# Six of eight conv channel tiles of an input projection as 2x2 block products, with attention results kept in DRAM

## The chip, the cores and the metric

The kernel runs on one core of a Trainium2 chip. The core has a matrix engine (TensorE, PE in the profile), three engines for elementwise work (VectorE is DVE, ScalarE is ACT, GpSimd is POOL), a synchronisation engine (SyncE, SP) that here only issues DMAs, an on-chip memory SBUF of 128 partitions, and PSUM, the matrix engine's accumulators. The metric is the device time of one execution in microseconds, lower is better.

## The reference

One layer of a hybrid decoder, in float32, for 512 tokens with 16 meta tokens put in front (L = 528), width 2048. What the change touches is the first half:

```python
n = _rmsnorm(h, g_mix[l])
p = n @ w_in[l]                      # 2048 -> 6 x 1024: q k v | b c u
q, k, v, gb, gc, u = jnp.split(p, ...)
o_attn = _stick_breaking_attention(norm(q), norm(k), v)   # 8 heads x 128
o_conv = gb * _causal_dwconv(gc * u, conv_w[l])           # 3 taps, 1024 channels
o = jnp.concatenate([_rmsnorm(o_attn, g_attn_out[l]),
                     _rmsnorm(o_conv, g_conv_out[l])], axis=-1)
h = h + o @ w_out[l]
n2 = _rmsnorm(h, g_ffn[l])
h = h + (jax.nn.silu(n2 @ w_gate[l]) * (n2 @ w_up[l])) @ w_down[l]
```

The FFN's inner width is 5632. The meta positions are dropped from the output.

## The kernel before, in words

**Layout and precision.** Activations are held transposed: 128 channels on the partitions, tokens along the row. A channel tile is 128 channels. To keep float32 precision on a faster matmul type, every operand is split into a high part (a cast to fp32r, on ScalarE) and a low part (the difference, on VectorE), and every product is three matmuls: high x high, high x low, low x high. So a weight block of 128 x 128 meets an activation of N tokens in three matmuls of N columns, and every weight passes once through ScalarE and once through VectorE.

**Input projection and attention.** x is scaled by g_mix and split into nh and nl, 16 tiles of 528 columns each (`split_x`, L236). `product` (L178, with `product_steps`, L162) runs over the 16 row tiles of one column tile of w_in, high and low weights from `next_w` (L141). `prepare` (L127) loads weights by SyncE, 1024 columns at a time into two buffers (raw), and splits 512 columns at a time into whi and wlo, four such pieces ahead. For each of eight heads (`head`, L337) the k, q and v column tiles are multiplied, and the attention of the head before is woven in: `after` (L151) puts a piece of work in a list, and `tick` (L154), called once per row tile, starts it when its count has run out. `mix` (L464) leaves a head's result, split, in its slot of oa, which stays in SBUF.

**Conv channels (L506 to L538).** For each of eight channel tiles j the column tiles c and u are multiplied for the tokens from 12 on (two halves of 258 columns, matmuls of 258) and b for the 512 real tokens (matmuls of 512). VectorE multiplies c by the square of the token's norm factor (L512), by u (L515), and adds the three taps (L517 to L522); b is scaled (L525), POOL multiplies (L526), and ScalarE and VectorE split the result into its slot of oc (L535, L536). The square is added up in acc_c for the norm.

**Output projection (L540 to L865).** The first output tile is multiplied with oa and oc by `product`; then the pools of the first half are released, and the pool sw is opened with other weight buffers: four of 1024 columns (b11, b12, b21, b22), three split pairs (s) and two sums. `wide_product` (L674) does the other 15 output tiles, and VectorE and POOL add the residual, build the FFN's activation blocks and store what does not fit. `scale_a` (L502) and `scale_c` (L775) turn the sums of squares into the two norm factors with two matmuls each (`token_scale`, L486).

**FFN as 2x2 blocks.** With the rows of a matrix in two halves, two column tiles, and the tokens in two halves, `pair_product` (L705) gets four block results from seven block products in place of eight. The activations come ready mixed in seven slots (f0 to f6, later ring and first); the weights' sums are made on the way: `prepare_pair` (L629) splits four blocks and three sums of blocks for the seven products and makes four additions of 1024 columns on VectorE (`add_quads`, L613). `block_product` (L685) is 8 row tiles x 3 matmuls of 256 columns; the results are combined from PSUM by three copies on ScalarE (L726 to L730) and three operations on VectorE (L732 to L739). 44 pairs make gate and up, 28 pairs the down projection (4 with 168 matmuls, 24 with 126).

**Order.** The code's order is only a start: the program is laid out by priority, so an engine's instructions may stand in another order than the code's, but each engine then runs its own list strictly in order. Weight preparation has high priority. All pools on the right side of SBUF are laid down from the top in the order in which they are opened: before, npool and wpool first, and after their release hpool (acc_h and 96 bytes named pad_h), sw, fpool (four of the f slots) and hbuf. A slot of activations starts 16 bytes into its tile.

Of the kernel before, what the change touches and what calls it, by code (L numbers as in the profile page):

```python
# [15 lines left out]
P = 128  # L16
# [17 lines left out]
def hybrid_layer(ctx: ExitStack, tc: tile.TileContext, xT, w_in, w_out, w_gu, w_down, vecs, out):  # L34
# [19 lines left out]
    tmp = open_pool("tmp", side="right")  # L54
# [5 lines left out]
    def t512(cols=SEQ, tag="t", bufs=6):  # L60
        n_tmp[0] += 1
        return tmp.tile([P, cols], F32, tag=tag, bufs=bufs, name=f"tmp{n_tmp[0]}")
# [39 lines left out]
    stream = []  # L102

    OUT_TILES = [k + 8 * half for k in range(8) for half in (1, 0)]

    def plan_w(src, n):
        stream.append((src, n))

    FIRST = ((0, 2), (2, 4), (4, 8), (8, 12), (12, 16))
    for a, b in FIRST:  # L110
        for c in (8, 0):
            plan_w(w_in[c, a // 8][:, (a % 8) * P : (a % 8 + b - a) * P], b - a)
    for j in range(HEADS):
        for c in (8 + j, j, 16 + j)[0 if j else 2 :]:
            for b in range(2):
                plan_w(w_in[c, b], 8)
    for j in range(HEADS):
        for c in (32 + j, 40 + j, 24 + j):
            for b in range(2):
                plan_w(w_in[c, b], 8)  # L120
    for b in range(2):
        plan_w(w_out[OUT_TILES[0], b], 8)
    raws, ready, taken = [], [], [0]
    SUB, AHEAD = 4, 4
    subs = [(i, a, min(a + SUB, n)) for i, (_, n) in enumerate(stream) for a in range(0, n, SUB)]

    def prepare():  # L127
        i, a, b = subs[len(ready)]
        with tc.high_priority():
            if i == len(raws):  # L130
                raws.append(wpool.tile([P, 8 * P], F32, tag="raw", bufs=2, name=f"raw{i}"))
                src, n = stream[i]
                nc.sync.dma_start(raws[i][:, : n * P], src)
            raw, c = raws[i][:, a * P : b * P], (b - a) * P
            hi = wpool.tile([P, SUB * P], F32R, tag="whi", bufs=AHEAD + 1, name=f"whi{i}_{a}")
            lo = wpool.tile([P, SUB * P], F32R, tag="wlo", bufs=AHEAD + 1, name=f"wlo{i}_{a}")
            sc.copy(hi[:, :c], raw)  # L137
            ve.tensor_tensor(lo[:, :c], raw, hi[:, :c].bitcast(F32), ALU.subtract)  # L138
        ready.append((hi, lo, b - a))

    def next_w():  # L141
        i = taken[0]
        taken[0] += 1
        while len(ready) < min(len(subs), i + 1 + AHEAD):
            prepare()
        hi, lo, n = ready[i]
# [936 lines left out]
```

## Time and profile before

| | |
|---|---|
| runs | 2111.97, 2111.64, 2109.75 us; median 2111.64 |
| profiled execution: span, first to last instruction | 2109.2 us (the page gives no other time of it) |
| granted TensorE clock, mean | 0.996 |
| instructions | 39231, of them 16086 matmuls |
| from HBM, to HBM | 268.60 MB, 71.30 MB |
| input projection and attention | about 0 to 347 us |
| conv channels | about 347 to 628.5 us |
| output projection | about 628.5 to 803 us |
| gate and up | about 805 to 1660 us |
| down projection | to the end |

How to read the rows: a name such as `pc<-nh,whi` is what an instruction writes and reads by the program's names (pk, pq, pv, pc, pu, pb are the projections' accumulators, po the output projection's, x, y, z those of the pairs). L512 is line 512 of the kernel. In the groups a row ends with the busy time, the mean length of one instruction in ns, and the idle time of its engine just before, with what ended it. Matmuls are pipelined, so their lengths overlap; the distance from start to start is what one costs.

### The profile page before, as it was taken

Reading aid. Unit: us, or ns where it says so; the run is one execution under the profiler, and the core shown is the slowest. Engines: PE = TensorE matmul, PEld = TensorE weight load, DVE = VectorE, ACT = ScalarE, POOL = GpSimd, SP = SyncE. Lnnn points to the kernel's source line nnn. Section 1 sums busy time; section 2 is a strip of 40 time slices with the busy share of each in tenths; the row PEclk is TensorE's granted clock in tenths of the full one; section 3 lists DMA queues with packets and bytes.
Section 4 is the critical chain, followed back from the end, with each engine's and each line's share of the span. In section 5 each row is a group of like instructions: output and inputs, shape, how many; then the busy total and the mean of one; then the engine's idle time right before and its main releaser. Section 6 shows DMA issues by size and latency. Waiting matters only on the chain.

```text
span 2109.2 us, 39231 instructions
## 1 busy us (share of the span) xinstructions
PE 2070.9 (98%) x16086; PEld 1989.7 (94%) x16086; DVE 1638.1 (78%) x2075; ACT 1013.5 (48%) x1532; POOL 470.2 (22%) x592
## 2 busy tenths in 40 slices
PE   8999999999999998999999999999999999999999
PEld 7999999999998888999999999999999999999999
DVE  8777767433337678899999998999989877776798
ACT  5666666322224344555544554554555544444443
POOL 4111111010013544122121121221111333122232
PEclk9999999999999999999999999999999999999999
DMA  5222222222235556566565565565554998788763
GB/s 173 80 71 80 71 80 81 81 93 98 91 113 170 180 181 215 166 183 192 156 185 170 152 193 166 164 182 158 171 155 145 319 298 244 218 244 242 222 191 120
DMA packets 147796, 342.47 MB, mean 162 GB/s; under 512 B 13136, under 2 KB 62800, under 8 KB 147616
## 3 DMA queue, kind: packets, MB, share of 16 engines
q1 hardware_dynamic: 69472, 216.17, 32.0%
q0 software_dynamic: 78144, 123.79, 21.9%
q8 instruction: 126, 2.06, 0.4%
q14 instruction: 54, 0.44, 0.1%
HBM read 268.60 MB, written 71.30 MB: 161 GB/s over the span
## 4 chain that ended last, share of the span: by engine, by line
PE 80%; DVE 8%; DMA 6%; issue 3%; ACT 2%; DVEq 0%; SPq 0%; ACTq 0%; POOL 0%
PE x L703 8%; PE x L701 8%; PE x L702 8%; DMA b<-w_down 4%; PE z L701 4%; PE z L702 4%; PE z L703 4%; DVE s L610 3%; PE po L681 3%; PE po L680 3%; PE po L682 3%; PE y L702 2%; PE y L703 2%; PE y L701 2%; PE pv L169 2%
## 5 line engine op out<-in xcount | busy, mean ns | idle before, releaser
L609 ACT CAST s<-t 128x1024 fp32r<-128x1024 f32 (+1 forms) x288 | 283.2, 983 | 403.5 <-PE x L703 132.3
L610 DVE TENSOR_TENSOR s<-t,s 128x1024 fp32r<-128x1024 f32 (+1 forms) x288 | 338.4, 1175 | 95.2 <-ACT s L609 94.7
L702 PE MATMUL x<-f,s 128*128 128x256 f32 x1408 | 388.1, 276 | 2.1 <-DVE f L184 1.3
L703 PE MATMUL x<-f,s 128*128 128x256 f32 x1408 | 388.1, 276 | 1.9 <-DVE s L610 1.9
L701 PE MATMUL x<-f,s 128*128 128x256 f32 x1408 | 388.1, 276 | 0.2 <-ACT f L183 0.2
L609 ACT CAST s<-b 128x1024 fp32r<-128x1024 f32 (+1 forms) x216 | 212.4, 983 | 217.5 <-PE x L703 196.1
L702 PEld LDWEIGHTS x<-f,s 128*128 128x128 f32 x1408 | 265.1, 188 | 2.5 <-DVE f L184 1.5
L703 PEld LDWEIGHTS x<-f,s 128*128 128x128 f32 x1408 | 265.0, 188 | 2.1 <-DVE s L610 2.1
L701 PEld LDWEIGHTS x<-f,s 128*128 128x128 f32 x1408 | 265.1, 188 | 0.5 <-ACT f L183 0.4
L610 DVE TENSOR_TENSOR s<-b,s 128x1024 fp32r<-128x1024 f32 (+1 forms) x216 | 245.5, 1137 | 5.6 <-ACT s L609 4.5
L138 DVE TENSOR_TENSOR wlo<-raw,whi 128x512 fp32r<-128x512 f32 (+1 forms) x198 | 142.3, 720 | 131.5 <-ACT whi L137 130.9
L896 POOL DMA_DIRECT2D fd<-s x147 | 104.1, 925 | 564.4 <-DVE s L184 562.9
L137 ACT CAST whi<-raw 128x512 fp32r<-128x512 f32 (+1 forms) x198 | 121.3, 614 | 186.7 <-PE pu L171 65.5
L701 PE MATMUL z<-f,s 128*128 128x256 f32 x704 | 195.8, 278 | 4.2 <-ACT sides L728 4.0
L703 PE MATMUL z<-f,s 128*128 128x256 f32 x704 | 193.9, 275 | 0.0
L702 PE MATMUL z<-f,s 128*128 128x256 f32 x704 | 193.9, 275 | 0.0
L616 DVE TENSOR_TENSOR t<-b,b 128x1024 f32<-128x1024 f32 (+1 forms) x144 | 165.1, 1146 | 36.2 <-DMA b<-w_down 32.8
L701 PE MATMUL x<-ring,s 128*128 128x256 f32 x608 | 168.5, 277 | 9.3 <-DVE d L736 5.7
L703 PE MATMUL x<-ring,s 128*128 128x256 f32 x608 | 168.0, 276 | 0.5 <-DVE s L610 0.5
L702 PE MATMUL x<-ring,s 128*128 128x256 f32 x608 | 167.5, 275 | 0.0
L701 PEld LDWEIGHTS z<-f,s 128*128 128x128 f32 x704 | 132.2, 188 | 7.4 <-ACT sides L728 7.4
L702 PEld LDWEIGHTS z<-f,s 128*128 128x128 f32 x704 | 132.2, 188 | 0.0
(350 smaller groups left out, 5695.3 us busy)
## 6 DMA issues: line engine op xcount, KB each, us to landing
b<-w_gu SPq DMA_DIRECT2D x176, 512.0 KB, 3.6
raw<-w_in SPq DMA_DIRECT2D x92, 512.0 KB, 3.4
fd<-s POOLq DMA_DIRECT2D x147, 256.0 KB, 5.3
b<-w_down SPq DMA_DIRECT2D x96, 384.0 KB, 4.8
ring<-fd POOLq DMA_DIRECT2D x42, 768.0 KB, 7.7
wide<-w_out SPq DMA_DIRECT2D x30, 512.0 KB, 3.7
hd<-d POOLq DMA_DIRECT2D x48, 256.0 KB, 7.7
b<-w_down SPq DMA_DIRECT2D x16, 512.0 KB, 7.6
```

The lines of the kernel that those rows point to most:

```text
L137: sc.copy(hi[:, :c], raw)
L138: ve.tensor_tensor(lo[:, :c], raw, hi[:, :c].bitcast(F32), ALU.subtract)
L609: sc.copy(hi, src)
L610: ve.tensor_tensor(lo, src, hi.bitcast(F32), ALU.subtract)
L616: ve.tensor_tensor(sums[name], a, b, ALU.add)
L680: pe.matmul(ps, hi[:, kk], ah, start=k == 0, stop=False)
L681: pe.matmul(ps, hi[:, kk], al, start=False, stop=False)
L682: pe.matmul(ps, lo[:, kk], ah, start=False, stop=k == 7)
L701: pe.matmul(p, hi[:, kk], act[:, 0, k], start=start and j == k == 0, stop=False, skip_group_check=skip)
L702: pe.matmul(p, hi[:, kk], act[:, 1, k], start=False, stop=False, skip_group_check=skip)
L703: pe.matmul(p, lo[:, kk], act[:, 0, k], start=False, stop=k == n - 1, skip_group_check=skip)
L896: gp.dma_start(fd[c][s][:, :, k], t[:, :, i])
```

## The change

Conv channel tiles 0 and 1 are multiplied as before (with 260 columns in place of 258). Tiles 2 to 7 go two at a time, as three pairs: (c, u) of the first, (c, u) of the second, (b, b) of both. Each is a `pair_product` over the 16 row tiles in two halves and the tokens from 8 on in two halves of 260, seven products of 8 row tiles.

The pairs need mixed activations. Three of the seven operands are parts of nh and nl as they are. Three blocks of differences (blk, split) are built during channel tile 1 by `form_blocks`, which loads x again; the seventh ("late") overwrites the second token half of the first eight nh and nl tiles after channel tile 1.

All weights of the kernel, from the first to the last, now pass through one plan and one set of buffers, those of sw, which is opened first: splits of 1024 columns, two ahead. The pool wpool and the reload between the two schemes go. Since blk and sw take the space that oa and oc had, each head's result and conv tiles 0 and 1 are written to DRAM when done (`stage_out`, one buffer), and loaded back by POOL's queue when blk has been read for the last time, in the last pair. The output projection starts with conv tiles 2 to 7 for two output tiles, then tiles 0 and 1, then the attention's eight. `scale_c` is handed to `after` ahead of these steps.

By the pools: hpool's pad_h (96 bytes) is gone, sw has a pad of 128 bytes at its lower end, hpool is opened below sw, and two tails of slots are shortened; the FFN's and the down projection's code is otherwise the same.

The diff, cut to its core:

```diff
+    sw = open_pool("sw", side="right")
+    sw.tile([P, 32], F32, name="pad_sw")
     npool = open_pool("npool", side="right")
-    wpool = open_pool("wpool", side="right")
...
+    CONV_FIRST = 2
+    def plan_pair(n, srcs, first=False):
+        i = len(pairs)
+        pairs.append((n, first))
+        for q in ("21", "11", "12", "22") if first else ("11", "12", "22", "21"):
+            loads.append(((i, q), n, srcs[("11", "12", "21", "22").index(q)]))
+        for s in (5, 0, 1, 2, 3, 4, 6) if first else range(7):
+            ents.append((i, s))
...
-    for j in range(HEADS):
+    for j in range(CONV_FIRST):
         for c in (32 + j, 40 + j, 24 + j):
             for b in range(2):
-                plan_w(w_in[c, b], 8)
+                plan_raw(w_in[c, b], 8)
+    for j in range(CONV_FIRST, HEADS, 2):
+        for c in ((32 + j, 40 + j), (33 + j, 41 + j), (24 + j, 25 + j)):
+            plan_pair(8, columns(c), not pairs)
...
+    S_AHEAD = 2
+    def split_quad(src, n):
+        t = sw.tile([P, 2, 8 * P], F32R, tag="s", bufs=S_AHEAD + 1, name=f"s{len(split_w)}")
+        hi, lo = (t[:, i, : n * P] for i in range(2))
+        sc.copy(hi, src)
+        ve.tensor_tensor(lo, src, hi.bitcast(F32), ALU.subtract)
...
+    def stage_out(name):
+        t = stage.tile([P, 2, SEQ], F32R, tag="st_o", name=f"st_{name}")
+        def store():
+            od[name] = dram.tile([P, 2, SEQ], F32R, name=f"od_{name}")
+            gp.dma_start(od[name], t)
+        return t[:, 0], t[:, 1], store
...
-    C0, CH = 12, (L - 12) // 2
+    C0, CH = 8, (L - 8) // 2
...
+            def form_blocks(k):
+                x4 = form.tile([P, 4, CH], F32, tag="x4", bufs=2, name=f"x4_{k}")
+                for i, kk in ((0, k), (2, k + 8)):
+                    nc.sync.dma_start(x4[:, i : i + 2], two(xT[kk][:, C0:]))
+                for i, kk in ((0, k), (2, k + 8)):
+                    sc.activation(x4[:, i : i + 2], x4[:, i : i + 2], AF.Copy, scale=g_mix[:, kk : kk + 1])
+                a11, a21, a12, a22 = (x4[:, i] for i in range(4))
+                ve.tensor_tensor(late[:, k], a11, a21, ALU.subtract)
+                ve.tensor_tensor(a22, a22, a21, ALU.subtract)
+                ve.scalar_tensor_tensor(a21, a22, -1.0, a11, ALU.mult, ALU.subtract)
+                ve.scalar_tensor_tensor(a12, a21, -1.0, a12, ALU.mult, ALU.subtract)
+                split(blk[:, :, 0, k], blk[:, :, 1, k], x4[:, 1:])
+            for k in range(8):
+                after(3 + 5 * k, lambda k=k: form_blocks(k))
...
+    for k in range(8):
+        hi, lo = (t[:, C0 + CH :] for t in n_hl[k])
+        split(hi, lo, late[:, k])
...
+    conv_acts = [
+        parts_of(0, C0), of_blk(2), of_blk(0), of_blk(1), parts_of(0, C0 + CH), parts_of(8, C0), parts_of(8, C0 + CH)
+    ]
...
+    def pair(acts):
+        c1, c2 = halves_of("e"), halves_of("e2")
+        x = pair_product(acts, two(c1), two(c2), sides)
+        sc.copy(two(c1)[:, 1], x)
+        return c1, c2
+
+    for j in range(CONV_FIRST, HEADS, 2):
+        ys = []
+        for m in range(2):
+            c1, c2 = pair(conv_acts)
+            ys.append(t512(SEQ, "v", 2)[:, :SEQ])
+            conv_taps(j + m, two(c1), two(c2), ys[m])
+        gbs = pair(conv_acts)
+        if j < HEADS - 2:
+            slots = [oc_mid[:, j + m - CONV_FIRST] for m in range(2)]
+        else:
+            cpool.release()
+            blk_pool.release()
...
+            with tc.high_priority():
+                for name, t in [(f"c{m}", oc_end[:, 2 + m]) for m in range(2)] + [(f"a{h}", oa_all[:, h]) for h in range(HEADS)]:
+                    gp.dma_start(t, od[name])
+        for m in range(2):
...
+            conv_out(j + m, gbs[m][:, META - C0 :], ys[m], slots[m][:, 0], slots[m][:, 1], s, gp if j < HEADS - 2 else ve)
+    oc_order = (*range(CONV_FIRST, HEADS), *range(CONV_FIRST))
...
-    hpool.tile([P, 24], F32, name="pad_h")
...
     after(3, scale_c)
+    steps = [wide_product(new_ps()[:, 1, :], oc, oc_order, 2) for _ in range(2)]
+    for _ in range(2):
+        for step in steps:
+            next(step)
+    for i in range(2):
+        run(wide_product(ps_out[i][:, 0, :], oa))
```

More of the change, by code (lines that the diff above doesn't have):

```diff
@@ L127, in prepare @@
     def prepare():
-        i, a, b = subs[len(ready)]
+        i, s = ents[len(split_w)]
         with tc.high_priority():
[L130 to L138, printed above, removed]
@@ L212, in hybrid_layer @@
     n_hl = []
[L213 removed]
+    accs = [pool.tile([P, L], F32, name=f"acc_x{i}") for i, pool in enumerate((rpool, atmp))]
     acc = accs[0]
@@ L543, in hybrid_layer @@
-    assert not waiting and len(ready) == taken[0] == len(subs)
-    rpool.release()
-    tmp.release()
-    const.release()
-    wpool.release()
-    npool.release()
-    hpool = open_pool("hpool", side="right")
-    sw = open_pool("sw", side="right")
-    acc_h = hpool.tile([P, SEQ], F32, name="acc_h")
-    hpool.tile([P, 24], F32, name="pad_h")
-    pairs = []
-    def gate_up(f):
-        return 8, [w_gu[n, f, k] for k in range(2) for n in range(2)]
-    def two_down(j, n):
-        return 2 * n, [
-            w_down[4 * j + m : 4 * j + m + 3 : 2, k, :, : n * P].rearrange("t p c -> p t c") for k in range(2) for m in range(2)
-        ]
```

439 lines of the change are left out of this document (233 added, 206 removed).

## The prediction, made before the changed kernel had run

> **What bounds the kernel now.** I read the page first, then the busy time by stage, then the rows of the products, then what stands around the joints the change makes.
>
> ```profile
> PE 2070.9 (98%) x16086; PEld 1989.7 (94%) x16086; DVE 1638.1 (78%) x2075; ACT 1013.5 (48%) x1532; POOL 470.2 (22%) x592
> ```
>
> TensorE is busy 98% of a span of 2109.2 us. The stages (columns: stretch, its length, then busy time and instructions of PE, weight load, DVE, ACT and POOL, granted clock, DMA share, GB/s):
>
> ```profile
> 0.00:40.00 40.00, 32.75 (x159) 27.99 (x160) 33.57 (x44) 24.59 (x43) 21.44 (x22) 0.87 0.59 189
> 40.00:347.00 307.00, 306.36 (x2105) 286.71 (x2104) 233.22 (x427) 192.55 (x353) 43.28 (x99) 1.00 0.24 78
> ...
> 390.00:628.50 238.50, 238.50 (x1669) 223.96 (x1669) 93.46 (x131) 65.59 (x106) 19.05 (x13) 1.00 0.30 98
> ...
> 639.50:803.00 163.50, 163.50 (x723) 135.35 (x722) 116.29 (x152) 65.14 (x105) 77.44 (x82) 1.00 0.58 175
> ...
> 830.00:1640.00 810.00, 805.79 (x7061) 802.55 (x7060) 736.90 (x798) 415.41 (x547) 151.06 (x198) 1.00 0.57 169
> ```
>
> The conv channels (390 to 628.5) leave TensorE no gap at all, and VectorE is busy 93 of 238 us there. So in this stage a matmul fewer is time saved, and VectorE has room. The FFN already works in 2x2 block products and shows what that costs: VectorE busy 737 of 810 us, and TensorE idle 4.2 us in all.
>
> A busy matmul of 0.28 us overlaps its neighbours, so I price matmuls by distance from start to start.
>
> ```profile
> 500.07 0.40 PE L169 MATMUL pc<-nh,whi 128*128 128x258 f32 x2
> ...
> 502.48 0.40 PE L171 MATMUL pc<-nl,whi 128*128 128x258 f32 x2
> ```
> ```profile
> 999.86 0.28 PE L702 MATMUL x<-f,s 128*128 128x256 f32 x1
> ...
> 1002.01 0.28 PE L703 MATMUL y<-f,s 128*128 128x256 f32 x1
> ```
>
> Between the first two lines lie ten rows of two: 2.41 us / 20 = 120.5 ns for 258 columns. Between the next two lie 19 matmuls: 2.15 / 19 = 113.2 ns for 256.
>
> **The conv products.** The VectorE row that takes each b product out of PSUM marks one channel tile per start:
>
> ```profile
> L525 DVE TENSOR_TENSOR tmp<-pb,r x8: 687/692/694, 390.1 to 628.6; 128x512 f32<-128x512 f32 x8
> ```
>
> Seven steps in 238.5 us are 34.07 us a tile, 204.4 us for tiles 2 to 7. The change puts nine pairs in their place (per two tiles: c and u of the one, c and u of the other, both b). A pair is 7 products x 8 row tiles x 3 matmuls = 168 matmuls of 260 columns. None of this width is in the trace; the nearest are
>
> ```profile
> L171 PE MATMUL pv<-nl,whi 128*128 128x264 f32 x256 | 51.6, 283 | 0.0
> L171 PE MATMUL pc<-nl,whi 128*128 128x258 f32 x256 | 51.5, 282 | 0.0
> ```
>
> which agree within 1 ns from both sides, so I take 120.5 ns: 9 x 168 x 0.1205 = 182.2 us. **Gain 22.2 us.** Bounds: 260/256 of the FFN's 113.2 (115.0) would give 30.5; 127 ns would give 12.4. Tiles 0 and 1 stay as they are, with 260 columns for 258: nothing.
>
> **Cover in the conv stage.** VectorE's price of a pair:
>
> ```profile
> L610 DVE TENSOR_TENSOR s<-t,s 128x1024 fp32r<-128x1024 f32 x192 | 239.1, 1246 | 66.2 <-ACT s L609 66.2
> ...
> L616 DVE TENSOR_TENSOR t<-b,b 128x1024 f32<-128x1024 f32 x96 | 119.2, 1241 | 3.5 <-DMA b<-w_down 1.0
> ...
> L732 DVE SCALAR_TENSOR_TENSOR u<-z,sides 128x256 f32<-128x256 f32 x44 | 18.5, 420 | 3.4 <-PE z L703 1.6
> ...
> L519 DVE SCALAR_TENSOR_TENSOR tmp<-tmp,vec,tmp 128x512 f32<-128x512 f32 x16 | 12.0, 752 | 1.6 <-ACT tmp L517 1.4
> ```
>
> 7 splits x 1.25 + 4 sums x 1.24 + 3 combinations x 0.42 = 15.0 us in 20.2 us of TensorE. The taps (two products by 0.69, two by 0.75) and the two outputs (two by 0.69, two by 0.75) add 2.9 us each: 53.7 of 60.7 us for two tiles, 88%, below the FFN's 91%. I cost it at nothing; the FFN lost 4.2 us in its stage of 42 pairs, 1 us for nine.
>
> The first pair is tighter. Its mixed blocks are formed during channel tile 1, whose stage was
>
> ```profile
> 594.30:628.40 34.10, 34.10 (x240) 32.01 (x240) 13.13 (x18) 9.13 (x15) 2.96 (x2) 1.00 0.40 136
> ```
>
> for the like tile 7. To 13.1 us of VectorE come, eight times, four operations of 260 columns and one subtraction of 780:
>
> ```profile
> L610 DVE TENSOR_TENSOR s<-b,s 128x768 fp32r<-128x768 f32 x72 | 68.5, 951 | 1.2 <-ACT s L609 0.3
> ...
> L808 DVE TENSOR_TENSOR src<-src 128x256 f32<-128x256 f32 x8 | 3.4, 425 | 5.5 <-ACT src L801 5.5
> ```
>
> 8 x (4 x 0.425 + 1.0) = 21.6 us, and acc_a's scale, six operations of at most 0.69: about 38 us in 34.1. The excess stands ahead of the first pair's splits, and the eight late halves (3.4 us), which wait for tile 1's last product to have read nh and nl, stand behind it. The mixed blocks are due at the third product, the late halves at the sixth, so part of it is slack: **2 us lost**, bounds 0 and 7.5. The sixteen loads of x behind the weights on SP's queue meet a DMA share of 0.30 and cost nothing. ScalarE, busy 9.1 us in that stage, has room for three more passes over each block.
>
> **Attention.** Its weights now come in splits of 1024 columns, fewer and longer, as far ahead as before; TensorE idled 0.6 us in 307, so nothing can be won. The eight stores stand on POOL, busy 43 of 307 us, ahead of only acc_a's addition: nothing. In the first 40 us TensorE waits for splits and x; four weight buffers for two put more weights ahead of the third x tile, but earlier: 0, bounds -2 and +2.
>
> **The joint to the output projection.** After the last b product ends, the old kernel did:
>
> ```profile
> 628.61 0.69 DVE L525 TENSOR_TENSOR tmp<-pb,r 128x512 f32<-128x512 f32 x1 [1.61 <-PE pb L173]
> 631.46 0.75 DVE L536 SCALAR_TENSOR_TENSOR oc<-tmp,vec,oc 128x512 fp32r<-128x512 f32 x1 [2.16 <-ACT oc L535]
> 634.09 0.69 DVE L184 TENSOR_TENSOR w<-acc_c,w 128x512 fp32r<-128x512 f32 x1 [1.88 <-ACT w L183]
> ```
> ```profile
> 629.38 1.29 POOL L526 TENSOR_TENSOR tmp<-tmp,tmp 128x512 f32<-128x512 f32 x1 [29.90 <-DVE tmp L525]
> ```
> ```profile
> L728 ACT COPY sides<-z 128x256 f32<-128x256 f32 x68 | 24.6, 362 | 0.0
> ```
>
> From the first start 3.6 us to the operand and 6.2 us to the split sum that scale_c multiplies, while TensorE had oa to work on. Now a copy (0.36) comes first and VectorE takes POOL's product (0.69 for 1.29): about 3.4 us, and TensorE begins with conv tiles 2 to 5, 12 matmuls x 0.227 = 2.7 us, then tiles 6 and 7. scale_c's two matmuls are handed in after three row tiles; where they stay there, everything behind them on TensorE waits until about 6 us. **1.5 us lost**, bounds 0 and 4.5.
>
> The ten tiles kept in DRAM come back by POOL's queue, 5.24 MB, released when blk is read for the last time, three products or 8.7 us ahead of the end. The first a tile is due after 48 matmuls of the projection, 10.9 us past the end, the last at 15.6. The nearest burst:
>
> ```profile
> L934 POOL DMA_DIRECT2D first<-fd x12: 701/732/816, 1643.7 to 1658.0; - x12
> ...
> DMA to landing us min/median/max: 4.4/13.0/17.8
> ```
> ```profile
> first<-fd POOLq DMA_DIRECT2D x12, 512.0 KB, 13.0
> ```
> ```profile
> 1660.00:1680.00 20.00, 19.51 (x170) 19.20 (x170) 19.14 (x21) 10.60 (x13) 2.52 (x3) 1.00 1.07 329
> ```
>
> Twelve such tiles were issued in 14.3 us and landed at the latest 17.8 later: at most 32 us, 2.7 us each, so ten take 27, ending 18 us past the end where 15.6 is due. TensorE lost 0.5 us in that burst. **1 us lost**, bounds 0 and 3.5.
>
> The Trainium skill, "SBUF — State Buffer", section "A bandwidth-pool intuition that's wrong (but worth ruling out)", says that a DMA issued from GpSimd waits for its descriptors while VectorE holds the port they share. By that rule these loads would be late beside a VectorE at 88%; in the burst above VectorE was busy 19.14 of 20 us and DMA still moved 329 GB/s, so the trace does not bear it out.
>
> **Where the weights lie.** sw is now the first pool of the right side, so nothing of uneven size stands above s. Before, hpool with its 96 bytes of pad_h stood there; whi and wlo had only pools of whole multiples of 64 bytes above. By the code's sizes s moves from 32 bytes off whi's place (modulo 64) onto it. Two sets of rows with the same operand oa and either weights:
>
> ```profile
> 630.04 0.39 PE L171 MATMUL po<-oa,whi 128*128 128x512 f32 x1
> ...
> 632.86 0.40 PE L171 MATMUL po<-oa,whi 128*128 128x512 f32 x1
> ```
> ```profile
> 694.77 0.39 PE L681 MATMUL po<-oa,s 128*128 128x512 f32 x1
> ...
> 697.49 0.39 PE L681 MATMUL po<-oa,s 128*128 128x512 f32 x1
> ```
>
> Twelve matmuls take 2.82 and 2.72 us: 235.0 and 226.7 ns. If that is the weights' place, 720 matmuls of the projection lose 8.3 ns each, 6 us; if not, 0. I take **3 us lost**. For the FFN and the down projection I take 0, bounds 0 and 120.5 - 113.2 = 7.3 ns a matmul: four of the seven f slots move down by the same 32 bytes (49280 + 2048 bytes above them for 2144 + 49152), and for short blocks the rows show no effect of the place (pv and pc start at other offsets of the same tiles, 283 and 282).
>
> The Trainium skill, "TensorE: Matmul & The Clock Gate", section "Step-by-step: what each phase is for", says that weights and the moving operand have read ports of their own, so that loading weights costs a running matmul no bandwidth. By it the 3 us would go too; 235.0 against 226.7 speaks against it as far as one operand can.
>
> **Sum.** -22.2 + 2 + 1.5 + 1 + 3 = -14.7 us: the span goes from 2109.2 to 2094.5. The page gives only the span of the profiled execution; the median run, 2111.6, lies 2.4 above, so I forecast **2097 us**.
>
> **Rivals.** (a) Slower: the weights' place counts in the 256-column products too. There are 44 x 168 + 4 x 168 + 24 x 126 = 11088 of them. By the ratio of the projection's rows (8.3 / 226.7 = 3.7%) each loses 4.1 ns, 46 us: 2143; at the upper bound 81 us: 2178. It decides from 14.7 us / 11088 = 1.3 ns a matmul. For it: the same operand at two prices. Against: the moved slots and the short rows. Chance 24%, and 6% that a smaller effect ends within 0.2% of before. (b) The joints cost their upper bounds (7.5 + 4.5 + 3.5 for 4.5: 11 us more): 2108; for it the 38 us in 34.1, against it the FFN's small idle time. Chance of most of it, around 2104: 12%. (c) The joints and the projection cost nothing, 7.5 us less: 2089.5, or less if 260 columns take under 120 ns. Chance 6%. The forecast, 2088 to 2103, has 52%.
>
> So faster by over 0.2% (what a measurement of this kernel can tell from no change) is 52 + 12 + 6 = 70%, within it 6%, slower 24%. The range, 2086 to 2145, takes in (b), (c) and the likelier half of (a).
>
> **What would show it.** The conv pairs: 168 matmuls in 20.2 us, with VectorE near 88% and no gap. The FFN's start-to-start still 113 ns; if it is 117 or more, (a) is right. A gap of 2 us in the first pair at the products that read blk. po rows between 227 and 235 ns, and no wait on oa's loads over 3 us. The forecast is wrong if 260 columns take 127 ns or if the 256-column products slow down.

## The result, and the profile after

The changed kernel takes **2129.6 us** (median of 4 runs, 2129.4 to 2130.5) against 2111.3 of the kernel before: 1.0090 times, 95% interval 1.0076 to 1.0105. The forecast was 2097. The kernel became 18 us slower where it should have become 15 us faster; the direction was that of rival (a).

The page after, busy time of the engines, and then the same stretches as before the change (length, busy time and instructions of PE, weight load, DVE, ACT, POOL, then granted clock, DMA share, GB/s):

```profile
PE 2087.8 (98%) x16158; PEld 2013.9 (95%) x16158; DVE 1736.1 (82%) x2121; ACT 1061.0 (50%) x1539; POOL 472.6 (22%) x610
```
```profile
0.00:40.00 40.00, 31.77 (x149) 25.61 (x149) 30.61 (x39) 22.58 (x38) 20.12 (x22) 0.91 0.67 214
40.00:347.00 307.00, 305.11 (x2086) 284.66 (x2086) 230.43 (x382) 188.52 (x308) 40.49 (x104) 1.00 0.27 89
424.00:445.00 21.00, 15.70 (x99) 14.23 (x99) 18.56 (x30) 11.64 (x18) 3.85 (x3) 0.89 0.33 107
445.00:625.80 180.80, 176.09 (x1426) 175.57 (x1426) 145.50 (x153) 80.59 (x107) 18.11 (x16) 0.97 0.33 111
639.50:807.00 167.50, 167.50 (x719) 134.84 (x719) 117.71 (x153) 64.75 (x104) 78.33 (x82) 1.00 0.55 172
840.00:1650.00 810.00, 809.76 (x6943) 807.69 (x6942) 726.49 (x788) 410.94 (x542) 148.01 (x192) 1.00 0.55 166
```

TensorE is as busy as ever, and that misleads. In the FFN's 810 us it stands for 0.2 us now, where it stood 4.2 before, and yet gets less done: 6943 matmuls recorded for 7061. In the conv pairs it has gaps (424 to 625.8) and a clock below 1, where the old stage had neither.

By the first matmul of each stage (both profiled executions; the span went from 2109.2 to 2128.8, +19.6):

| stage | before | after | difference |
|---|---|---|---|
| start and attention, to the first conv product | 347.4 | 350.9 | +3.5 |
| conv tiles 0, 1 | 75.5 | 75.5 | 0 |
| conv tiles 2 to 7 | 205.5 | 199.4 | -6.1 |
| output projection | 174.9 | 181.3 | +6.4 |
| gate and up | 856.3 | 872.1 | +15.8 |
| down projection, to the end of the span | 449.6 | 449.6 | 0 |

The prediction had 204.4 us for the old tiles 2 to 7. It took them from seven starts of the VectorE row L525, the first of which, at 390.1 us, came 2 us after TensorE had begun the next product (388.15); by TensorE's own starts they took 205.5.

So two things have to be explained: why the pairs gave 6 us and not 22, and why stages whose products the change leaves as they were take 22 us more.

**The untouched stages: each matmul takes longer.** Timeline rows of the output projection, twelve matmuls apart, and of the FFN, 24 apart:

```profile
693.68 0.40 PE L808 MATMUL po<-oc_end,s 128*128 128x512 f32 x1
...
696.48 0.40 PE L808 MATMUL po<-oa,s 128*128 128x512 f32 x1
```
```profile
999.90 0.28 PE L711 MATMUL x<-f,s 128*128 128x256 f32 x1
...
1002.70 0.28 PE L711 MATMUL z<-f,s 128*128 128x256 f32 x1
```

2.80 / 12 = 233.3 ns for 226.7 before, and 2.80 / 24 = 116.7 for 113.2. The start-to-start distance of the FFN's matmuls, averaged by product, differs by the slot that the product reads: 117.1 to 117.4 ns with f0, f1, f2 and f5, 114.7 to 115.2 with f3, f4 and f6. All slots are read alike; what sets f3, f4 and f6 apart is where they lie (the change moved the other four).

**The pairs: gaps, and half clock behind them.** TensorE's rows with idle time ahead of them, in the first pair and once in the fourth (it comes back at 569.4 in the seventh):

```profile
432.97 0.39 PE L711 MATMUL z<-blk,s 128*128 128x260 f32 x1 [0.66 <-ACT tmp L645]
438.62 0.38 PE L711 MATMUL z<-blk,s 128*128 128x260 f32 x1 [2.84 <-ACT blk L273]
439.62 0.39 PE L712 MATMUL z<-blk,s 128*128 128x260 f32 x1 [0.62 <-DVE blk L274]
441.30 0.58 PE L711 MATMUL x<-blk,s 128*128 128x260 f32 x1 [1.18 <-ACT sides_c L737]
```
```profile
504.65 0.39 PE L711 MATMUL x<-blk,s 128*128 128x260 f32 x1 [2.35 <-ACT sides_c L737]
```

The gaps are 5.3 + 2 x 2.35 = 10.0 us. What ScalarE did around the fourth pair's, and what it waited for on POOL:

```profile
503.09 0.72 ACT L627 ACTIVATE oc<-tmp,vec 128x512 fp32r<-128x512 f32 x1 [2.61 <-POOL tmp L625]
503.72 0.61 ACT L292 ACTIVATE sq<-tmp 128x512 f32<-128x512 f32 x1
504.24 0.35 ACT L737 COPY sides_c<-x 128x260 f32<-128x260 f32 x1
```
```profile
500.88 2.18 POOL L625 TENSOR_TENSOR tmp<-tmp,tmp 128x512 f32<-128x512 f32 x1 [6.03 <-DVE tmp L624]
```

ScalarE runs its list in order. The activation that splits the conv result waits 2.61 us for POOL's product, and behind it stands the copy that empties x, for which TensorE's next product waits. Then the clock:

```profile
502.30:504.65 2.35, 0.00 (x1) 0.00 (x1) 2.35 (x2) 1.50 (x3) 0.93 (x2) 1.00 0.00 0
504.65:506.50 1.85, 1.85 (x11) 1.85 (x12) 0.16 (x1) 0.52 (x1) 1.29 (x1) 0.66 0.64 188
506.50:509.90 3.40, 3.40 (x22) 3.40 (x22) 2.28 (x2) 1.88 (x4) 1.29 (x1) 0.68 0.13 54
509.90:513.30 3.40, 3.40 (x31) 3.40 (x30) 2.07 (x3) 1.81 (x3) 0.00 (x0) 1.00 0.17 30
```

Shortly after the gap the granted clock is halved, by the trace's clock record for 3.41 us (6.83 in the first pair, 3.41 at the other two): 13.65 us at half speed lose 6.8 us. 182.2 us of matmuls, 10.0 of gaps and 6.8 of slow clock are 199.0 of the 199.4. The Trainium skill, "TensorE: Matmul & The Clock Gate", section "HAM oscillation — how this bites in real kernels", asks for no idle gap over about 3.4 us; here 2.35 us was enough. It isn't always: in the run below with only the weights moved, a gap of 2.22 us at the same place (503.7 us) was followed by full clock, and the next one of 2.23 us (567.4) by 3.41 us at half.

### The profile page after: what moved, and what is told of

It reads as the page before. It is cut to its first block, busy times and chain, and to the rows that moved or that the text cites. A ratio compares the mean times of both kernels' runs of the same rounds, so it can differ in the third digit from the quotient of the medians.

```text
span 2128.8 us, 39398 instructions
## 1 busy us (share of the span) xinstructions
PE 2087.8 (98%) x16158; PEld 2013.9 (95%) x16158; DVE 1736.1 (82%) x2121; ACT 1061.0 (50%) x1539; POOL 472.6 (22%) x610
## 4 chain that ended last, share of the span: by engine, by line
PE 86%; DVE 5%; DMA 5%; issue 2%; ACT 1%; POOL 0%; SPq 0%; DVEq 0%; ACTq 0%; POOLq 0%
PE x L711 12%; PE x L713 12%; PE x L712 12%; PE z L711 6%; PE z L712 6%; PE z L713 6%; PE y L711 3%; PE y L713 3%; PE y L712 3%; PE po L808 3%; PE po L810 3%; PE po L809 3%; DMA b<-w_down 3%; DVE s L177 2%; PE pv L259 2%
## 5 line engine op out<-in xcount | busy, mean ns | idle before, releaser
L176 ACT CAST s<-t 128x1024 fp32r<-128x1024 f32 (+1 forms) x324 | 320.2, 988 | 453.1 <-PE z L713 151.4
L176 ACT CAST s<-b 128x1024 fp32r<-128x1024 f32 (+3 forms) x341 | 337.7, 991 | 353.3 <-PE x L713 266.4
L177 DVE TENSOR_TENSOR s<-t,s 128x1024 fp32r<-128x1024 f32 (+1 forms) x324 | 384.1, 1185 | 123.3 <-ACT s L176 122.9
L177 DVE TENSOR_TENSOR s<-b,s 128x1024 fp32r<-128x1024 f32 (+3 forms) x341 | 403.4, 1183 | 53.7 <-ACT s L176 50.4
L713 PE MATMUL x<-f,s 128*128 128x256 f32 x1408 | 392.6, 279 | 4.2 <-DVE s L177 4.2
L712 PE MATMUL x<-f,s 128*128 128x256 f32 x1408 | 393.1, 279 | 2.0 <-DVE f L274 1.3
L711 PE MATMUL x<-f,s 128*128 128x256 f32 x1408 | 392.8, 279 | 0.1
L183 DVE TENSOR_TENSOR t<-b,b 128x1024 f32<-128x1024 f32 (+1 forms) x162 | 187.2, 1155 | 23.8 <-DMA b<-w_down 19.4
L711 PE MATMUL x<-ring,s 128*128 128x256 f32 x608 | 170.2, 280 | 5.3 <-DVE d L747 3.6
L713 PE MATMUL x<-ring,s 128*128 128x256 f32 x608 | 169.7, 279 | 0.1
L712 PE MATMUL x<-ring,s 128*128 128x256 f32 x608 | 169.6, 279 | 0.0
L711 PEld LDWEIGHTS z<-f,s 128*128 128x128 f32 x704 | 132.3, 188 | 2.3 <-ACT sides L739 2.2
L712 PEld LDWEIGHTS z<-f,s 128*128 128x128 f32 x704 | 132.4, 188 | 0.0
L713 PEld LDWEIGHTS z<-f,s 128*128 128x128 f32 x704 | 132.4, 188 | 0.0
L711 PEld LDWEIGHTS x<-ring,s 128*128 128x128 f32 x608 | 114.2, 188 | 6.6 <-ACT s L176 3.7
```

Of the source, the lines that this page charges most:

```text
L176: sc.copy(hi, src)
L177: ve.tensor_tensor(lo, src, hi.bitcast(F32), ALU.subtract)
L183: ve.tensor_tensor(sums[name], a, b, ALU.add)
L711: pe.matmul(p, hi[:, kk], act(0, k), start=start and j == k == 0, stop=False, skip_group_check=skip)
L712: pe.matmul(p, hi[:, kk], act(1, k), start=False, stop=False, skip_group_check=skip)
L713: pe.matmul(p, lo[:, kk], act(0, k), start=False, stop=k == n - 1, skip_group_check=skip)
```

## The experiments

Theory P: the distance between matmuls is set by where their operands lie in SBUF, and the change moved them. Rival T: the lists of ScalarE and VectorE are mixed otherwise, and places don't matter. All addresses below are worked out from the code's pools and tiles; the stage times are read from each run's profiled execution as in the table above.

**Weights back to a multiple of 64.**

```diff
+    top = open_pool("top", side="right")
+    top.tile([P, 8], F32, name="pad_top")
     sw = open_pool("sw", side="right")
-    sw.tile([P, 32], F32, name="pad_sw")
+    sw.tile([P, 24], F32, name="pad_sw")
```


> The changed kernel with its split weights moved by 32 bytes, from 32 past a multiple of 64 bytes to a multiple of 64, as the stages from the out-projection on had them before; the slots of the FFN's activations stay where the change put them, 16 past a multiple of 64 where they were at 48 past it. Theory P (the place of the operands sets the pitch of the matmuls, and the change lost 15.8 us in gate/up and 6.4 in the out-projection by it): the out-projection's pitch falls back from 233.3 to 226.7 ns, 5 us; gate/up falls from about 117 ns to between 113.4 and 116, by 7 to 15.8 us; so 2107 to 2118 us, and up to 10 us less if the 2664 half-row products of the in-projection, which took 120.5 ns in both kernels with weights at 32 past 64, gain 4 ns each as well. Rival T (the pitch is longer because the splits and loads of one list run at other times; places do not matter): no stage moves by over 1 us, 2129 to 2131 us. Rival F (only the place of the FFN's activations counts): the out-projection and gate/up stay, 2129 to 2131 us.

Measured: 2128.6 us (2124.7 to 2134.2), ratio to the kernel before 1.0093, interval 1.0067 to 1.0119. The output projection fell to 176.2 us, as P says; gate/up did not fall (874.8). Its products with f3, f4 and f6 went up to 118.3 ns, the others down to 115.2. T is out for the projection; P as stated is out for the FFN.

**Slots back.** In each of `pad(fpool, 160)`, `pad(first, 11936)` and `pad(rings_p[1], 160)` 32 bytes less.

> The changed kernel with the FFN's activation slots and the down-projection's right-hand rings moved up by 32 bytes, to 48 past a multiple of 64 bytes as before the change; the weights stay 32 past a multiple of 64. In the changed kernel's trace the gate/up products that read slots at 48 past 64 have a mean pitch of 114.7 to 115.2 ns, those that read slots at 16 past it 117.1 to 117.4. Theory P: all go to about 114.9, so 5280 matmuls of gate/up gain 2.4 ns each, 12 us, the out-projection stays at 233 ns, the down-projection gains nothing or a few us: 2113 to 2119 us. Rival T (order, not place): no change, 2129 to 2131 us. Rival W (only the weights' place counts): no change either, but the weights-only run then falls by the whole 20 us.

Measured: three runs at 2137.9 to 2139.5 us and the profiled one at 2119.2; ratio 1.0116, interval 1.0071 to 1.0162. P's 2113 to 2119 was missed by all but the profiled one, which lies at its upper end. In the profiled one all products have 115.3 to 115.6 ns on average, but no single matmul stream has: stretches of 113.3, 116.7 and 118.7 follow one another, and change at small stalls. Two windows of 28 us on either side of such a stall (at 1199.0 one matmul starts 176 ns behind the last):

```profile
1170.00:1198.00 28.00, 28.00 (x239) 28.00 (x238) 25.67 (x28) 14.73 (x20) 5.99 (x8) 1.00 0.54 163
1202.00:1230.00 28.00, 28.00 (x249) 28.00 (x249) 24.98 (x28) 13.82 (x17) 4.27 (x7) 1.00 0.58 174
```

Both are full, at full clock, with the same operands and much the same work beside them: 239 and 249 matmuls (the first two in each began earlier: 28 / 237 = 118.1 and 28 / 247 = 113.4 ns). So in some places a stream has several possible distances. That the three slower runs ran at the longer ones is likely but not shown, since they left no trace.

**Both back.**

> Both moves together: weights at a multiple of 64 bytes, slots and right-hand rings at 48 past it, the places that these stages had before the change. Theory P: gate/up back to 856 us and 113.4 ns, the out-projection back to 175 or 176 (its 1.3 us gap stays), the down-projection between 445 and 450; 2107 to 2110 us, and up to 10 us less if the in-projection's products gain as well. Rival T: 2129 to 2131 us.

Measured: 2136.1 us (2134.9 to 2143.1), 1.0133, interval 1.0110 to 1.0156. A miss by 27 us: gate/up 885.8 us, with 275 of 281 groups of 24 matmuls (from 840 to 1640 us) at 118.5 ns to the nearest half, although weights and slots were where they had been before, modulo 64. The projection was at 176.4.

**The place alone, on the kernel before.**

```diff
-    hpool.tile([P, 24], F32, name="pad_h")
+    sw.tile([P, 24], F32, name="pad_sw")
```


> The kernel before, with nothing of the change but the place: the split weights of the out-projection, gate/up and down moved by 96 bytes, to 32 past a multiple of 64; the FFN's slots stay at 48 past it. Theory P: the out-projection's 768 matmuls at 233 ns for 226.7, 5 us more; gate/up at 114.7 to 115.2 for 113.4, 7392 times 1.3 to 1.8 ns, 10 to 13 us more; down between nothing and 6.6 us more (its idle time may take it up): 2125 to 2135 us. Rival T (order, not place): no change, 2110 to 2113 us.

Measured: 2144.7 us (2143.6 to 2152.1), 1.0179, interval 1.0152 to 1.0205: projection 180.4, gate/up 881.3, with nothing of the change in it. T is out: moving the weights by 96 bytes costs the old kernel 36 us, and P's 2125 to 2135 us is missed by 10.

**A finer grain.** Sorted by remainders of 128 bytes the runs agreed with one another (weights 0 with slots 112 in the kernel before, 64 with 112 in the run with both moved back). So the next run put both to the old remainders, with the three slot paddings 32 bytes shorter as above; another moved only the weights.

```diff
+    top.tile([P, 24], F32, name="pad_top")
...
+    sw.tile([P, 8], F32, name="pad_sw")
```


> The changed kernel with its split weights at a multiple of 128 bytes (96 bytes lower than the change put them) and the FFN's slots and right-hand rings at 112 past it: the remainders by 2048 that both had before the change. In the runs so far each pair of remainders by 128 had its own pitches of FFN matmuls: weights 0 with slots 112 (the kernel before) 113.3 ns in 257 of 274 groups of 24; weights 64 with slots 112 118.3 ns in all 275; weights 96 with slots 112 a mixture of 113.3, 116.7 and 118.7. Theory Q (the remainder by 128, not by 64, sets what pitches a matmul can have): gate/up at 113.3 to 113.6 ns and 853 to 858 us, the out-projection 175 to 176.5, down 446 to 451, and 2105 to 2111 us, up to 10 us less if the in-projection's 120.5 ns fall too. Rival L (a lottery of the stalls' moments, in which places have no part): a mixture as in the other runs, 2119 to 2140 us. Rival A (what counts is how the lists of ScalarE and VectorE are mixed now): gate/up over 116 ns, 2125 us or more.

Measured: **2107.6 us** (12 runs, 2103.9 to 2112.1), 0.9981, interval 0.9972 to 0.9990. Timeline rows 24 matmuls apart, 2.73 / 24 = 113.8 ns with the joint of two products between them:

```profile
999.27 0.28 PE L713 MATMUL z<-f,s 128*128 128x256 f32 x1
...
1002.00 0.28 PE L713 MATMUL x<-f,s 128*128 128x256 f32 x1
```

Gate/up is back at 857.2 us. Nothing but paddings differs from the changed kernel, and 22 us are gone. The projection stayed at 178.0, 2 us over the expectation, and the input projection gained nothing: from the first pv to the first conv product 307.1 us for 305.5.

> Only the weights to a multiple of 128 bytes; four of the seven FFN slots, and the right-hand rings, stay where the change put them, 80 past it. Theory Q: the two products of a pair that read the slots at 112 past it have 113.3 ns; what the pair of weights 0 with slots 80 has isn't known, 113.3 to 118.7, so gate/up between 854 and 878 us and the kernel between 2105 and 2130. Rival W (the weights' place alone counts): 113.3 in all products and the same time as the run with both moved, within 3 us. Rival L: 2119 to 2140 us.

Measured: 2128.6 us, 1.0088, interval 1.0076 to 1.0100: products with f3, f4 and f6 at 113.4 to 113.9 ns, those with the other four slots at 119.8. So what counts is the two places together, not the weights' alone.

**The places by themselves.** A kernel of matmuls only, weights and data at all steps of 32 and 16 bytes.

```python
for t in range(times):
    for k in range(8):
        wh, wl = (w[:, wo + i * 1024 + k * P :][:, :P] for i in range(2))
        ah, al = (d[:, do + (i * 8 + k) * stride :][:, :cols] for i in range(2))
        ...
```


> Leaves out the whole computation (the output is zeros) and measures the pitch of matmuls by themselves: 128x128 fp32r weights at 0, 32, 64 and 96 bytes past a multiple of 128, data of 256, 260 and 512 columns at 0, 16, ... 112 bytes past it, in the FFN's order of high and low parts, 48 matmuls to a group, each group behind a short wait for the eviction of the last; no other engine writes meanwhile but that eviction. Theory Q (the two remainders by 128 alone set the pitches a stretch can have): for 256 columns, weights 0 with data 112 at 113.3 ns in every repeat; 64 with 112 at 118.3; 96 with 112 at 113.3, 116.7 or 118.7; 0 with 80 up to 119.8; 96 with 80 about 117. Rival K (the pitch grows by a collision with what ScalarE and VectorE write while they split weights, and places only matter for that): all groups at 113.3 within 0.5 ns.

Measured: distances from 113.3 to 120.0 ns for 256 columns, with no other engine at work but for one eviction after each group. Rival K is out. Two groups (least, median and greatest length in ns, first and last start in us), with the same weights and the data 16 bytes apart:

```profile
L62 PE MATMUL wb_db<-d,w x16: 275/275/281, 67.5 to 72.6; 128*128 128x256 f32 x16
```
```profile
L62 PE MATMUL wb_da<-d,w x16: 279/282/286, 41.7 to 47.1; 128*128 128x256 f32 x16
```

From the first start to the last are 45 matmuls: 5.1 / 45 = 113 ns and 5.4 / 45 = 120 ns (113.8 and 119.9 by the finer start times). But remainders by 128 were not enough either: 113.8 came with weights 32 and data 16, weights 64 and data 48, weights 96 and data 80, not with 0 and 112 (117.2). Sorted by **data address minus weight address, modulo 256**, the groups fall into line (means in ns from the trace's start times, for some of the differences; below each line what the whole kernels had there):

```
difference       0      16          48     64           80     112    128          160          192    224    240
256 columns      -      -           118.4  113.3,117.8  118.3  113.8  118.6-120.0  117.3-118.6  117.8  118.2  117.2
 whole kernels   -      113.3-118.7 118.3  -            119.8  113.3  -            -            -      -      117.2
260 columns      -      -           119.0  118.8        119.6  120.0  120.0        121.0        119.0  120.0  120.1
512 columns      -      -           -      228.8        -      -      231.9-233.3  234.3        233.3  232.9  -
 whole kernels   226.7  -           -      228.9        -      -      233.3        234.3        233.3  233.3  -
```

This is Theory R. The data blocks of 260 columns lie 1152 bytes apart, so a group of that width takes two differences, 128 apart, in turn; it stands under the difference of its first block. That the difference counts modulo 128 is out (64 against 192, 112 against 240). That it repeats after 256 bytes rests on the whole kernels: f0 and f1 lie 16640 bytes apart, 65 times 256, and had the same distance. The difference alone doesn't settle everything: at 64 each pair of places kept its own distance in all three repeats, 117.8 ns with weights at 64 and 113.3 with weights at 96.

The changed kernel had 224 in the projection and 240 or 16 in the FFN, the kernel before 0 and 112.

**Theory R forecasts.** The weights of the kernel before 64 bytes up (`pad_h` 8, and a `pad_sw` of 16 in sw); and, below, the results of attention and conv.

> The kernel before with nothing changed but the place of the weights of the out-projection and the FFN: 64 bytes up (acc_h goes up with them). Theory R: the FFN's difference goes from 112 to 48, where the changed kernel with weights at 64 had 118.35 ns in every stretch: gate/up 880 to 886 us for 856; the out-projection's from 0 to 192, where the run of the places alone had 233.3 ns for 512 columns: 179.5 to 181 us for 174.9; down between nothing and 5 us more: 2140 to 2150 us, 1.015 to 1.019 of the kernel before. If the weights have to stand at a remainder other than a multiple of 64 to cost anything (as forecast in the first instance), or if the change's lists are needed for it: no change, 2107 to 2113 us.

Measured: 2143.8 us (2141.7 to 2147.4), 1.0167, interval 1.0145 to 1.0188; gate/up 882.7, projection 179.7, both inside what R gave beforehand. 276 of 281 groups of 24 (840 to 1640 us) have 118.5 ns to the nearest half:

```profile
999.29 0.28 PE L704 MATMUL x<-f,s 128*128 128x256 f32 x1
...
1002.13 0.28 PE L704 MATMUL z<-f,s 128*128 128x256 f32 x1
```

**POOL's product to VectorE**, with the places mended.

```diff
-            conv_out(j + m, ..., slots[m][:, 1], s, gp if j < HEADS - 2 else ve)
+            conv_out(j + m, ..., slots[m][:, 1], s, ve)
-        conv_out(j, gb, y, oh, ol, t512(SEQ, "e", 2)[:, :SEQ])
+        conv_out(j, gb, y, oh, ol, t512(SEQ, "e", 2)[:, :SEQ], ve)
```


> As the run with both places at the old remainders by 128, and the conv product b times y of tiles 0, 1 and of the first two pairs of tiles on VectorE in place of GpSimd (it was there for the last two tiles already). Theory H (ScalarE runs its list in order, so its copy of x for the pair's next product stands behind the oc activation, which waits 2.6 us for GpSimd's 2.2 us product; TensorE then stands 2.35 us twice and 2.8 us once, and runs at half clock for 3.4 us twice and 6.8 us once afterwards): the two 2.35 us gaps go with their half-clock windows, 8 us; in the first pair the 2.8 us gap shrinks to under 1 us, up to 5 us more with its window; the conv tiles 2 to 7 take 186 to 191 us for 199, and the kernel is 8 to 13 us faster than the run with the places alone. Rival V (VectorE, at 80% there, gets late instead, since it takes four products of 0.7 us more): the gaps stay within 1 us of theirs, the kernel within 2 us.

Measured: **2098.8 us** (2096.7 to 2099.8), 0.9946, interval 0.9934 to 0.9958, 8.8 us less than with the places alone. The stretches without and with this edit:

```profile
428.00:445.00 17.00, 11.85 (x82) 10.68 (x81) 14.56 (x24) 9.91 (x16) 3.86 (x3) 0.92 0.38 124
445.00:619.00 174.00, 169.54 (x1359) 169.00 (x1358) 140.77 (x147) 76.81 (x103) 14.28 (x8) 0.97 0.32 101
```
```profile
428.00:445.00 17.00, 12.38 (x85) 11.67 (x84) 17.00 (x27) 9.81 (x15) 3.81 (x2) 0.84 0.46 152
445.00:619.00 174.00, 173.94 (x1431) 173.38 (x1430) 147.44 (x158) 80.62 (x107) 10.24 (x12) 1.00 0.35 114
```

From 445 on TensorE is full and at full clock: both gaps and both half-clock windows went, as theory H says. The first pair kept its gap (2.5 us at the last block, where H had under 1), and VectorE is now busy 17.00 of 17 there. The pairs take 190.8 us. The time lies near the forecast of 2097, but by other terms: against the kernel before (profiled executions), the start and the attention cost 4.8 us, the pairs gave 14.7, the projection cost 3.1, and the down projection gave 6.6 that nobody had forecast.

**The start.** On top of that, the third and fourth weight buffer loaded later.

```diff
-        if not a:
+        if b == KT:
             load_next("b12")
             load_next("b22")
```


> As the run with the places and the product on VectorE, and the third and fourth weight buffer get their first load only after the last x tile is asked for, so that as in the kernel before two weight tiles are on their way during the start. Theory B (the first 45 us are bound by the loads; the changed kernel moves 1.05 MB more of weights in them, ahead of x, at about 300 GB/s 3.4 us): the first matmul of pv comes at 42 to 43 us for 45.4, and the kernel is 2 to 3.5 us faster than the run without this. Rival C (not the loads but ScalarE's and VectorE's lists set the start): within 1 us.

Measured: 2100.4 us (2095.0 to 2103.2), 0.9953, interval 0.9939 to 0.9967. pv starts at 41.7 us for 45.1, as theory B says, but the first conv product at 351.3 for 352.2. TensorE's waits in the first 100 us without and with the edit (total, times, longest):

```profile
PE pk L263 <- DVE nl L336: 5.4, 6, 1.6
PE pk L261 <- ACT nh L333: 3.1, 3, 1.4
```
```profile
PE pq L265 <- DVE s L179: 4.0, 3, 2.1
PE ss_q L427 <- DVE sl_q L276: 2.1, 1, 2.1
PE pk L263 <- DVE nl L336: 1.6, 2, 1.3
```

The waits for x turned in part into waits for split weights. The loads are the cause of the late pv; but of the 3.4 us won, 2.5 were lost again before the first conv product, and the kernel became no faster.

**Blocks earlier, results at 128.** `after(3 + 5 * k` became `after(1 + 4 * k`, and accpool got a pad of 64 bytes.

> As the run with the places and the product on VectorE, with two more edits in stages of their own. First, the eight block formations are set at every fourth k tile from the first instead of every fifth from the third, so that the last is due nine k tiles, 3 us, earlier. Theory D (the first pair's wait of 2.5 us for the last block, and the 0.7 and 1.4 us behind it, end with it): the first pair's gaps fall from 4.6 us to under 2, and with the half-clock window behind them (6.8 us at half) the stage is 4 to 6 us shorter. Rival E (VectorE is busy 17 of 17 us there, and the block's formation waits for it or for x's transfers, not for its place in the list): gaps within 1 us of before. Second, the attention and conv results go up by 64 bytes, to a multiple of 128 as in the kernel before: by theory Q the out-projection falls from 178.0 us to 175 or 176; by rival W (the weights' place alone counts) it stays at 178.

Measured: 2104.4 us (12 runs, 2098.3 to 2106.4), 0.9969, interval 0.9957 to 0.9981. Theory D falls, E holds; the first pair's gap is the same to 0.02 us:

```profile
438.66 0.39 PE L714 MATMUL z<-blk,s 128*128 128x260 f32 x1 [2.53 <-ACT blk L275]
```

And the projection went up, from 178.0 to 181.3, against theory Q: the difference had become 128.

**Results at 0.** The pad of accpool 192 bytes instead.

> As the run with the places and the product on VectorE (blocks formed at their old points again), and the attention and conv results moved up by 192 bytes. Theory R, formed after the run that measured the places alone: what counts is the data's address minus the weights', modulo 256 bytes. For 512 columns that run had 228.8 ns at a difference of 64 and 231.9 to 233.3 at 128; the whole kernels had 226.7 at 0 (the kernel before), 178.0 us of out-projection at 64 and 181.3 at 128. Here the difference is 0: out-projection 175 to 176.5 us, so 1.5 to 3 us less than with the difference at 64, and 2095 to 2098 us. By theory Q as it stood (each remainder by 128, here the same as in the run with the results 64 bytes up) it would stay at 181, and 2102 to 2105 us.

Measured: 2099.7 us (2096.2 to 2102.4), 0.9953, interval 0.9938 to 0.9968. The projection is at 176.3, as R gave beforehand (226.7 ns, the group's rows at 389 for 392 to 398):

```profile
L813 PE MATMUL po<-oa,s x117: 389/389/389, 639.8 to 789.4; 128*128 128x512 f32 x117
L811 PE MATMUL po<-oa,s x116: 389/389/389, 640.0 to 788.9; 128*128 128x512 f32 x116
```

The 1.7 us did not show in the total: the down projection took 446.8 us for 443.0 in the profiled execution, for which no cause was sought. The two versions can't be told apart in time.

## Why the prediction was wrong, point by point

- **Gain in the pairs, 22.2 us.** 1512 matmuls at 120.5 ns were right: where there is no gap, 168 matmuls take 20.2 us (from the fourth pair's y at 514.87 to the fifth's at 535.09), 120.4 ns each. The stage gave 6.1, and 14.7 with the product on VectorE; the rest is in the next two points.
- **Cover in the conv stage, "nothing".** This step failed by 8.1 us: two gaps of 2.35 us, and 1.7 lost at half clock behind each. VectorE's load was priced nearly rightly (88% forecast; 145.5 of 180.8 us is 80%, and 147.4 of 174 in the run without these gaps 85%), but the price of the stage was not VectorE's. ScalarE's list holds the copies that empty PSUM behind an activation that waits for POOL. The kernel before had that wait too (row of ScalarE's waits in its conv stage: total, times, longest), but there VectorE emptied PSUM, and nothing that TensorE needed soon stood behind it. The rows were there to be seen before the forecast:

```profile
ACT oc L535 <- POOL tmp L526: 15.1, 7, 2.8
```

- **First pair, 2 us (0 to 7.5).** The place was right, the products that read blk; the gaps were 5.3 us and the half clock 3.4 more: 8.7, over the upper bound, since the bound had no clock in it.
- **Attention 0, start 0 (-2 to +2).** Attention was right: 305.4 and 305.5 us from the first pv to the first conv product. The start cost 3.4, over its bound; the loads of two more buffers stood ahead of x, as the run with later loads showed.
- **Joint to the projection, 1.5 us:** a gap of 1.27 us. **Results from DRAM, 1 us:** no wait. Both lie inside their bounds.
- **Weights' place in the projection, 3 us (0 to 6).** 768 x 6.6 ns = 5.1, inside. The rows behind it, 235.0 and 226.7 ns with the same oa, were of differences 160 and 0, where the matmuls alone gave 234.3 and the whole kernels 226.7: a good reading, with the wrong rule (64 bytes, and one operand) made of it.
- **Weights' place in the FFN, 0 (0 to 7.3 ns a matmul).** This step turned the sign: 15.8 us in gate/up, and nothing in the down projection, whose matmuls also took 117 ns, but whose idle time shrank by the 8.3 us that these rows, before and after, show of 390 (3696 matmuls at 3.2 ns more are 12 us; where the rest went stays open):

```profile
1700.00:2090.00 390.00, 373.38 (x3218) 369.20 (x3217) 304.18 (x373) 175.49 (x268) 106.40 (x116) 1.00 0.80 226
```
```profile
1700.00:2090.00 390.00, 381.67 (x3234) 379.97 (x3234) 303.03 (x364) 177.11 (x268) 110.58 (x129) 1.00 0.84 238
```

  The zero had two reasons, and both failed. The first, that four of the seven slots move by the same 32 bytes as the weights, holds modulo 64 only: by the code's sizes the weights went up by 96 bytes and these slots down by 32, so the difference went from 112 to 240, and for f3, f4 and f6, which stayed, to 16. At 112 the whole kernels had 113.3 ns, at 240 117.2. The second, pv and pc at the same price from different offsets, was read from products that mix differences: the nh and nl tiles are 2112 bytes long, so within one product the difference takes eight values (four by the tile, 64 apart, times two token halves), and a mean over the product can hardly show one of them. Alone, groups of 260 columns, which mix two differences, vary by 2.2 ns, those of 256 at a single difference by 6.7.
- **Rival (a)** had the mechanism and the sign. Its 46 us took every one of 11088 matmuls as 4.1 ns dearer; in gate/up they were about 3 dearer (by the two prices above, four slots and three), a part of that was idle time before, and the down projection paid nothing on balance.
- **The Trainium skill's rule** of separate read ports ("TensorE: Matmul & The Clock Gate", "Step-by-step: what each phase is for") was set against one pair of rows. The run of matmuls alone speaks against its consequence: with nothing else reading, 16 bytes between two places of the data made 113.8 or 119.9 ns. What in the memory or its paths collides was not shown.

Open: why the difference counts modulo 256, and which distance a stream takes where there are several (16, 64, 144, 160). At 16, in the run with the slots moved, it changed at stalls; that the moment of the restart decides is argued, not shown. Not tried: to take the first pair's work off VectorE, whose list is full there.

## What to carry to other kernels

When an edit moves tiles in SBUF, work out the address of the moving data minus that of the weights, modulo 256, for every stage that reads them, the untouched ones too (shown here for fp32r with weights loaded anew for every matmul), and compare start-to-start distances before and after: a share of busy time can't show it. When results are taken out of PSUM by copies, look at what stands ahead of each copy in its engine's list, since the wait of one unrelated activation can become a gap on TensorE and then a stretch at half clock. Test evidence against an effect on the same shape, at the same single address difference, that would pay for it.

## What the runs showed of the hardware that was not expected

- In the run of matmuls alone, fp32r matmuls of 256 columns take 113.3 to 120.0 ns by the places of their operands, those of 512 228.8 to 234.4 (226.7 in whole kernels at a difference of 0), those of 260, over two differences each, 118.8 to 121.0.
- After a stall of some 60 ns the next 335 matmuls stood 113.3 ns apart for 118.7 before it.
- A gap of 2.35 us in a full stream was followed by 3.41 us at half clock, one of about 5 us in parts by 6.83; one of 2.22 us by none.
